# One unit's products walk their 512 columns in other orders

## The chip, the cores and the metric

The kernel runs on one core of a Trainium2 chip. The core has a matrix engine (TensorE, PE in the profile, with its weight loads as PEld), VectorE (DVE), ScalarE (ACT), GpSimd (POOL) and SyncE (SP), which here only issues loads and stores. The metric is the device time of one execution in microseconds (us); lower is better.

## The reference

The input is one sequence of 256 positions with 4096 features. The reference computes one layer and a last norm:

```python
xn = rms_norm(x, norm_attn)
q, k, v, g = split(xn @ w_in, 4)            # w_in: 4096 x 16384, 32 heads of 128
z = q @ k.T * scale                          # strictly causal
a = exp(log_sigmoid(z) + suffix sums of log_sigmoid(-z))
h = x + ((a @ v) * silu(g)) @ w_out          # w_out: 4096 x 4096
out = rms_norm(h, final_norm)
```

Nearly all of the work is in the two large products, xn @ w_in and the one with w_out. The convolution layer named in the reference's description isn't reached, since it runs for a depth of one.

## The kernel before, in words

**Units and steps.** The columns of w_in are cut into sixteen units (u = 0 to 15) of 1024 columns each: two blocks of 256 for q and k, two for gate and v. Four more units do w_out. A unit runs over the 4096 rows of the weights in sixteen steps (s = 0 to 15) of two chunks of 128 rows. In one step, a 2 x 2 block product has to be made: two halves of the rows of x, two chunks of the sum, and two groups of 512 columns.

**Seven or eight products.** Unit 0 makes eight products in each step. In every other unit the steps in `SEVEN` (1, 3, 4, 6, 7, 9, 10, 12, 13, 14) use a scheme of seven products with sums and differences of blocks, and the others (0, 2, 5, 8, 11, 15) use eight. So a unit after the first has 10 x 7 + 6 x 8 = 118 products. The results are gathered in seven accumulators of the PSUM memory (tiles `acc`, 128 partitions x 512 columns of fp32, one bank each), which stay open over the sixteen steps of a unit.

**A product is three matmuls.** An operand in fp32 is split into a high part, rounded to the format fp32r, and the remainder, also fp32r. `mm3` (line 762) then issues high x high, high x low and low x high, all into the same accumulator. The stationary operand, 128 x 128, is a part of x (tiles `sh`, `sl`; for w_out `oh`, `ol`); the moving operand, 128 x 512, is a part of the weights (tiles `wh`, `wl`). `mm3` is called by `product` (line 1185), which looks up the accumulator, the form of x and the piece of the weights.

**What feeds it.** SP loads the raw weights by 256 KB into seven buffers (`raw`), POOL adds a chunk onto some of them by a DMA that accumulates, VectorE makes further sums there, ScalarE writes `wh` (`piece`, line 426), and VectorE writes `wl`. In memory the 512 columns of `wh` and `wl` lie next to each other, in straight order, as do those of an accumulator. The buffers of `wh` and `wl` are returned when the product that used them last is done.

**The heads.** The attention of unit u's two heads (`head`, line 777) runs during the first seven steps of unit u + 1. Its matmuls (tiles `tr`, `z`, `o`) stand between the products in TensorE's order; at some places they are plain fp32, at others fp32r.

**What sets the order.** A planner written in the kernel (`Plan`, line 102) simulates the five engines with fixed costs while the program is built, and writes the instructions out in the order that comes of it. It reckons a product at three matmuls of `tensor_ns(512)`, whatever its operands look like. The order is therefore fixed before the kernel runs; on the chip the engines wait for one another by semaphores.

Of the kernel before, what the change touches and what calls it, by code (L numbers as in the profile page):

```python
# [84 lines left out]
def plain_part(k, one, two):  # L85

    return k, BOTH, ((one, "A11", 0), (two, "A21", 0), (one, "A12", 1), (two, "A22", 1))


def vector_ns(n):  # L90
# [147 lines left out]
def kernel(  # L238
# [41 lines left out]
    for u, (kind, w, cols) in enumerate(units):  # L280
        for s in (step_at(u, k) for k in range(NS)):
            quads.append(tuple((w, c, s) for c in cols))
            if kind == "plain":
                which = [plain_part(0, PLAIN["C11"], PLAIN["C21"]), plain_part(1, PLAIN["C12"], PLAIN["C22"])]
            else:
                which = SEVEN_PARTS if s in SEVEN and not (u == LAST and s in EIGHT_LAST) else EIGHT_PARTS
            for i, (k, place, prods) in enumerate(which):
                parts.append(
                    dict(u=u, s=s, i=i, tile=(len(quads) - 1, k), place=place, prods=prods, quad=len(quads) - 1,
                         seven=which is SEVEN_PARTS, size=place.stop - place.start)  # L290
                )
# [8 lines left out]
    for g, (n, k) in enumerate(order):  # L300
        p = parts[n]
        b = p["u"], p["prods"][k][0]
# [456 lines left out]
        nc.give("qkl")  # L759
        nc.tell(("gate", u))  # L760

    def mm3(out_, a, b, start, stop):

        (ah, al), (bh, bl) = a, b
        kw = dict(skip_group_check=True)
        nc.tensor.matmul(out_, ah, bh, start=start, stop=False, **kw)
        nc.tensor.matmul(out_, ah, bl, start=False, stop=False, **kw)
        nc.tensor.matmul(out_, al, bh, start=False, stop=stop, **kw)
# [416 lines left out]
    def product(n, k):  # L1185
        p = parts[n]
        b, f, c = p["prods"][k]
        h, l = forms[p["s"]]
        mm3(
            ev[p["u"]][b],  # L1190
            (h[:, PLACES[f], :], l[:, PLACES[f], :]),
            (wh[n][:, c, :], wl[n][:, c, :]),
            starts[p["u"], b] == (n, k),
            ends[p["u"], b] == (n, k),
        )

    def products():
        for g, (n, k) in enumerate(order):
            p = parts[n]
            u, s = p["u"], p["s"]  # L1200
            b, f, c = p["prods"][k]
            if u < 1:
                what = "s"
            elif u < OUT0:
                what = "n"
            elif u == OUT0:
                what = "o"
            else:
                what = "r" if u == LAST and s in EIGHT_LAST else "p"
            if starts[u, b] == (n, k):  # L1210
                yield nc.take(f"b{b}")
                ev.setdefault(u, {})[b] = acc.tile([P, W], F32, tag=f"b{b}", name=f"acc{u}_{b}")
            yield nc.until(("low", n, c), ("form", what, s), lead=nc.LEAD)
            yield nc.work(
                "tensor", PRODUCT, lambda: product(n, k), g * PRODUCT, after=lambda n=n, k=k: done(n, k), hold=False
            )
            nc.here = g * PRODUCT
# [59 lines left out]
```

## Time and profile before

| what | value |
|---|---|
| median of 3 runs | 1740.17 us (1738.72 to 1741.6) |
| span of the profiled execution | 1738.8 us |
| TensorE busy | 1722.9 us (99%) |
| VectorE busy | 1643.5 us (95%) |
| ScalarE busy | 1204.9 us (69%) |
| GpSimd busy | 335.5 us (19%) |
| mean granted TensorE clock | 0.998 |
| DMA | 413.79 MB, mean 238 GB/s |

For the profiled execution the page has the span, from the first to the last instruction, and no other time; it lies at the low end of the three runs. Busy time counts an engine's records. The records of matmuls overlap, since matmuls are pipelined: one of 512 columns is drawn with 389 ns, but they start closer together. What a matmul costs TensorE is therefore read from the distance between starts, or from a stretch that holds a known number of them. Nearly every instruction carries line 121, which is the helper that records it; groups are told apart by their tiles.

### The profile page before, as it was taken

How to read it: one execution, taken by the hardware profiler on the slowest of the kernel's cores; microseconds unless marked ns; L12 is line 12 of the kernel's file. 1: busy time of each engine (PE TensorE's matmuls, PEld its weight loads, DVE VectorE, ACT ScalarE, POOL GpSimd, SP SyncE). 2: the span in 40 equal slices, each digit the busy share in tenths (PEclk: the TensorE clock that was granted, in tenths of full speed). 3: DMA queues.
4: the chain of work that ended last, by engine and by line, in shares of the span. 5: the costliest groups of instructions: out<-in, count | busy, mean ns of one | idle time of the engine just before them, and what ended most of it. 6: DMA issues, size and time to landing. Idle time of an engine off the chain costs nothing.

```text
span 1738.8 us, 24830 instructions
## 1 busy us (share of the span) xinstructions
PE 1722.9 (99%) x7735; PEld 1412.5 (81%) x7735; DVE 1643.5 (95%) x2106; ACT 1204.9 (69%) x1640; POOL 335.5 (19%) x407
## 2 busy tenths in 40 slices
PE   9999999999999999999999999999999999999997
PEld 6888888888888888888888888888888888878885
DVE  8889999999999999999999999999999987999997
ACT  7976767676767676767676767676767675666655
POOL 0022222222222221212222222222222112221220
PEclk9999999999999999999999999999999999999999
DMA  9967788878787878787878787878787878788895
GB/s 363 297 191 227 229 231 226 230 229 236 224 234 223 240 216 238 217 251 208 255 206 255 206 256 198 257 203 259 198 256 203 269 245 265 230 268 251 233 303 191
DMA packets 249380, 413.79 MB, mean 238 GB/s; under 512 B 28128, under 2 KB 73440, under 8 KB 249248
## 3 DMA queue, kind: packets, MB, share of 16 engines
q1 hardware_dynamic: 194544, 354.24, 60.6%
q0 software_dynamic: 54416, 57.70, 20.2%
q8 instruction: 60, 0.98, 0.2%
q14 instruction: 72, 0.59, 0.1%
q10 hardware_dynamic: 288, 0.28, 0.0%
HBM read 403.98 MB, written 8.13 MB: 237 GB/s over the span
## 4 chain that ended last, share of the span: by engine, by line
PE 78%; DVE 12%; issue 6%; ACT 2%; DMA 2%; SPq 0%; DVEq 0%; ACTq 0%
PE acc L121 74%; DVE wl L121 8%; DVE raw L121 3%; PE z L121 2%; PE o L121 1%; ACT wh L121 1%; DMA raw<-in_w_in_dram 1%; PE tr L121 1%; DVE gv_sb L121 1%; DVE h L121 0%; DMA raw<-in_w_out_dram 0%; DMA grow<-in_gain_out_dram 0%; DVE qk_sb L121 0%; SPq L121 0%; ACT sq L121 0%
## 5 line engine op out<-in xcount | busy, mean ns | idle before, releaser
L121 ACT CAST wh<-raw 128x1024 fp32r<-128x1024 f32 (+1 forms) x995 | 922.0, 971 | 406.1 <-issue 180.0
L121 DVE TENSOR_TENSOR wl<-raw,wh 128x1024 fp32r<-128x1024 f32 (+1 forms) x995 | 1068.8, 1123 | 58.4 <-ACT wh L121 56.6
L121 PE MATMUL acc<-wh,sh 128*128 128x512 f32 x1898 | 755.6, 398 | 0.0
L121 PE MATMUL acc<-wl,sh 128*128 128x512 f32 x1898 | 740.0, 390 | 0.8 <-DVE wl L121 0.8
L121 PE MATMUL acc<-wh,sl 128*128 128x512 f32 x1898 | 740.5, 390 | 0.0
L121 POOL DMA_DIRECT2D raw<-in_w_in_dram x300 | 262.9, 988 | 1078.9 <-DMA raw<-in_w_in_dram 427.4
L121 PEld LDWEIGHTS acc<-wh,sl 128*128 128x128 f32 x1898 | 356.3, 188 | 75.8 <-DVE sl L121 0.4
L121 PEld LDWEIGHTS acc<-wl,sh 128*128 128x128 f32 x1898 | 357.0, 188 | 73.8 <-DVE wl L121 2.8
L121 PEld LDWEIGHTS acc<-wh,sh 128*128 128x128 f32 x1898 | 356.8, 188 | 70.7 <-ACT wh L121 0.6
L121 DVE TENSOR_TENSOR raw<-raw,raw 128x512 f32<-128x512 f32 x354 | 243.4, 687 | 6.9 <-DMA raw<-in_w_out_dram 1.2
L121 PE MATMUL acc<-wl,oh 128*128 128x512 f32 x485 | 189.7, 391 | 2.0 <-DVE wl L121 1.8
L121 PE MATMUL acc<-wh,oh 128*128 128x512 f32 x485 | 190.0, 392 | 0.0
L121 PE MATMUL acc<-wh,ol 128*128 128x512 f32 x485 | 188.9, 389 | 0.0
L121 DVE TENSOR_TENSOR raw<-raw 128x512 f32<-128x512 f32 x177 | 121.0, 684 | 0.0
L121 PEld LDWEIGHTS acc<-wl,oh 128*128 128x128 f32 x485 | 91.1, 188 | 23.8 <-DVE wl L121 5.3
L121 PEld LDWEIGHTS acc<-wh,oh 128*128 128x128 f32 x485 | 91.0, 188 | 19.2 <-DVE gv_sb L121 0.5
L121 PEld LDWEIGHTS acc<-wh,ol 128*128 128x128 f32 x485 | 91.0, 188 | 18.8
L121 POOL DMA_DIRECT2D raw<-in_w_out_dram x54 | 47.1, 968 | 185.9 <-DVE wl L121 58.9
L121 ACT ACTIVATE f<-f 128x384 f32<-128x384 f32 x96 | 50.5, 526 | 3.0
L121 ACT COPY qkT<-tr 128x512 f32<-128x512 f32 x32 | 18.6, 581 | 24.1 <-PE tr L121 24.1
L121 ACT CAST oh<-p 128x512 fp32r<-128x512 f32 (+3 forms) x46 | 20.9, 467 | 18.8 <-DVE p L121 13.2
L121 DVE SCALAR_TENSOR_TENSOR gv_sb<-acc,rin_v,gv_sb 128x512 f32<-128x512 f32 x45 | 33.4, 741 | 0.0
(91 smaller groups left out, 750.3 us busy)
## 6 DMA issues: line engine op xcount, KB each, us to landing
raw<-in_w_in_dram SPq DMA_DIRECT2D x1024, 256.0 KB, 4.5
raw<-in_w_out_dram SPq DMA_DIRECT2D x256, 256.0 KB, 4.3
raw<-in_w_in_dram POOLq DMA_DIRECT2D x300, 128.0 KB, 4.7
p<-spill POOLq DMA_DIRECT2D x28, 256.0 KB, 4.2
raw<-in_w_out_dram POOLq DMA_DIRECT2D x54, 128.0 KB, 5.1
xr<-in_x_dram SPq DMA_DIRECT2D x16, 256.0 KB, 4.8
xres<-in_x_dram SPq DMA_DIRECT2D x16, 256.0 KB, 5.6
out_dram<-h SPq DMA_DIRECT2D x16, 256.0 KB, 2.8
```

The costliest lines, as they stand in the source:

```text
L121: return self.tc.keep_in_program_order(getattr(self.engine, name)(*args, **kw))
```

## The change

The matmuls of one unit of w_in, unit 5, go over their 512 columns in another order. `WALKS` gives fourteen of the sixteen steps a pattern (h, e); steps 0 and 5 have none. `mm3` cuts the 512 columns into h equal parts, and each part into runs of e columns. The walk takes the first run of each part in turn, then the second run of each, and so on. The moving operand and the accumulator are both walked so, and each column of the product is added where it was added before. What lies in memory, and the stationary operand, stay as they are.

For pattern (2, 2), for example, the columns come as 0, 1, 256, 257, 2, 3, 258, 259 and so on; for (2, 128) as 0 to 127, 256 to 383, 128 to 255, 384 to 511.

```diff
+WALKED = 5
+WALKS = {
+    1: (2, 16), 2: (2, 8), 3: (2, 4), 4: (2, 2), 6: (2, 32), 7: (2, 64), 8: (2, 128),
+    9: (4, 16), 10: (8, 16), 11: (16, 16), 12: (32, 4), 13: (4, 4), 14: (8, 4), 15: (4, 64),
+}
...
-    def mm3(out_, a, b, start, stop):
+    def mm3(out_, a, b, start, stop, walk=None):
 
         (ah, al), (bh, bl) = a, b
+        if walk:
+            h, e = walk
+            out_, bh, bl = (t.rearrange("p (h i e) -> p i h e", h=h, e=e) for t in (out_, bh, bl))
         kw = dict(skip_group_check=True)
         nc.tensor.matmul(out_, ah, bh, start=start, stop=False, **kw)
         nc.tensor.matmul(out_, ah, bl, start=False, stop=False, **kw)
...
             starts[p["u"], b] == (n, k),
             ends[p["u"], b] == (n, k),
+            WALKS.get(p["s"]) if p["u"] == WALKED else None,
         )
```

## The prediction

> **What bounds the kernel now.** I read the page first: the engine totals, the slices, and the chain of work that ended last.
>
> ```profile
> span 1738.8 us, 24830 instructions
> PE 1722.9 (99%) x7735; PEld 1412.5 (81%) x7735; DVE 1643.5 (95%) x2106; ACT 1204.9 (69%) x1640; POOL 335.5 (19%) x407
> PEclk9999999999999999999999999999999999999999
> PE 78%; DVE 12%; issue 6%; ACT 2%; DMA 2%; SPq 0%; DVEq 0%; ACTq 0%
> ```
>
> TensorE is busy 99% of the span at the full granted clock, and 78% of the chain is its own work. VectorE, at 95%, is close behind, so I have to see which of the two sets the pace in the edited unit. I found unit 5 by counting products in program order: unit 0 has 128, every later input unit 118, each three matmuls. The windows view for units 4, 5 and 6, and then for steps 7 to 15 of unit 5 (columns: length, then busy time and instructions of each engine, granted clock, DMA share, GB/s):
>
> ```profile
> core 0: us, PE busy (x) PEld busy (x) DVE busy (x) ACT busy (x) POOL busy (x), PEclk, DMA share, GB/s
> 353.26:439.37 86.11, 86.11 (x391) 70.81 (x391) 82.96 (x103) 60.48 (x80) 18.24 (x22) 1.00 0.82 230
> 439.37:525.43 86.06, 86.06 (x391) 70.81 (x391) 82.93 (x103) 60.43 (x80) 18.01 (x21) 1.00 0.80 228
> 525.43:611.57 86.14, 86.14 (x391) 70.82 (x391) 82.98 (x103) 60.41 (x80) 17.95 (x22) 1.00 0.82 230
> 480.54:525.43 44.89, 44.89 (x199) 37.12 (x198) 42.69 (x50) 28.63 (x35) 10.97 (x13) 1.00 0.85 252
> ```
>
> Unit 5 takes 86.06 us, like its neighbours, and in it TensorE is never idle while VectorE has 3.1 us to spare. The waits inside unit 5 that concern TensorE are these (total us, times, longest):
>
> ```profile
> PEld z L121 <- DVE fl L121: 0.3, 1, 0.3
> PEld o L121 <- ACT gated L121: 0.3, 1, 0.3
> PEld tr L121 <- DVE gated L121: 0.2, 1, 0.2
> PEld o L121 <- issue: 0.2, 1, 0.2
> ```
>
> All of them belong to attention heads, and together they are 1.0 us; no product waits for its weights. The chain over the unit, with start, length and content of each piece, gives the price of a matmul:
>
> ```profile
> 21 pieces in order of time: start us, us, what
> ...
> 443.41 12.28 PE acc L121 x54
> ...
> 462.69 0.44 PE tr L121 x4
> ...
> 480.04 46.04 PE acc L121 x203
> ```
>
> The last row is 203 matmuls back to back: 46.04 / 203 = 226.8 ns for one walk over 512 columns. That pitch, not the 389 ns by which a record is drawn, is the price. So a nanosecond put on a matmul here is a nanosecond on the end.
>
> **The change part by part.** No instruction is added, removed or moved: in the lists of the two built kernels the only rows that differ, on any engine, are 306 matmuls of unit 5, which carry shapes such as 128x128x2x2 in place of 128x512. So no DMA, semaphore, queue or buffer changes its place. Each pattern (h, e) walks 512 columns as runs of e neighbours, going round h places that lie 512/h columns apart; operand and accumulator walk alike, so the sums are the same. Steps 0 and 5 have no pattern. Of the other fourteen, ten have 7 products (21 matmuls) and four (2, 8, 11, 15) have 8 (24 matmuls): 210 + 96 = 306, and 306 x 226.8 = 69.4 us of the path are touched.
>
> By run length: e = 2 in step 4 (21 matmuls, 256 runs each); e = 4 in steps 3, 12, 13, 14 (84 matmuls, 128 runs); e = 8 in step 2 (24, 64 runs); e = 16 in steps 1, 9, 10, 11 (87, 32 runs); e = 32, 64, 128 in steps 6, 7, 15, 8 (90, of 16 to 4 runs). That is 5,376 + 10,752 + 1,536 + 2,784 + 792 = 21,240 runs.
>
> The trace has no TensorE row whose moving operand or accumulator jumps. The nearest rows:
>
> ```profile
> L121 DVE TENSOR_TENSOR raw<-raw 128x512 f32<-128x512 f32 x177 | 121.0, 684 | 0.0
> L121 DVE TENSOR_TENSOR h<-acc,h 128x512 f32<-128x512 f32 x19 | 12.5, 681 | 0.0
> L121 PEld LDWEIGHTS acc<-wh,sl 128*128 128x128 f32 x1898 | 356.3, 188 | 75.8 <-DVE sl L121 0.4
> L121 PE MATMUL tr<-ident,qk_sb 128*128 128x128 f32 x128 | 19.2, 272 | 0.0
> ```
>
> On VectorE the first row reads and writes two runs of 256 columns that lie apart, the second one straight run out of the accumulator: 684 against 681 ns. A jump after a long run costs at most 3 ns there. That is the lower end, and I take it (as nothing) for long runs, e of 16 to 128. The LDWEIGHTS row says that the next weights take 188 of the 226.8 ns and lie beside the stream; they are read straight as before, and a slower stream only hides them better.
>
> The upper end is a stream at half rate. The last row is a transpose of plain fp32, 128 columns; four of them, in the chain above (tr x4), take TensorE 0.44 us, which is 440 ns for 512 columns, 213 ns more than the fp32r walk. I use it for whatever may feed or accept only half as much. A gain is bounded too: if these fp32 columns take the array two cycles, one cycle is 0.43 ns, 512 of them 220 ns, and the fp32r walk loses 6.8 ns to something else. Were a jump to remove that everywhere, it would give 306 x 6.8 = 2.1 us.
>
> Is there a limit near? Short fp32r streams stand in the timeline of a head:
>
> ```profile
> 455.53 0.33 PE L121 MATMUL z<-fh,neg_tri 128*128 128x384 f32 x1
> 455.70 0.34 PE L121 MATMUL z<-fl,neg_tri 128*128 128x384 f32 x1
> 455.88 0.22 PE L121 MATMUL z<-fh,neg_tri 128*128 128x128 f32 x1
> 455.94 0.28 PE L121 MATMUL z<-fl,neg_tri 128*128 128x128 f32 x1
> ```
>
> From start to start, 384 columns take 0.17 us and 128 columns 0.06: about 0.44 to 0.47 ns a column at every length, so the walk is paid by the column and not by the instruction. A stream that is slightly slower than the array's own 0.43 looks like one held by what feeds 4-byte columns. If that feed comes in pieces of a few columns, runs shorter than a piece waste part of it. The width of a piece is in no row. I choose that it is wider than 2 and not wider than 4: step 4, with the shortest runs, gets the half-rate row, and all others the row of the free jump, which they resemble more. The sum: 21 x (440 - 227) = 4.5 us in step 4, 0 elsewhere.
>
> [...]
>
> Nothing covers the 4.5 us: TensorE is the path in unit 5. What is late next gains slack: the splits on ScalarE and VectorE, the loads on SP's queue and the adding loads on POOL's are released by products of the same order, somewhat later, and then have 4.5 us more. At most the 1.0 us of waits above can come back inside the unit; I count none. Unit 6 has no idle TensorE either, so it gives nothing back. The sum on the profiled execution is 1738.8 + 4.5 = 1743.3 us. Its span is at the low end of the three runs (1738.72, 1740.17, 1741.6); on their median, 1740.17, it is 1744.7 us.
>
> **The rivals.** *No walk costs anything (the other side).* The place is step 4: if the feed delivers any aligned pair at full rate, the 4.5 us are gone, and the time is 1740.2 us, or down to 1738.1 with the bound of the gain. It decides from a pitch in step 4 under about 390 ns (3.5 us in 21 matmuls, which is 0.2%). For it speaks the 684 against 681; against it, that this row has a jump in 256 columns and runs at 1.3 ns a column, a third of TensorE's demand.
>
> *Short runs cost more widely.* If a piece is 8 columns, e = 4 falls to half rate too: 105 matmuls x 213 = 22.4 us, 1762.5 us. If every run costs one column's time (0.443 ns), 21,240 x 0.443 = 9.4 us, 1749.6 us. For it: the 6.8 ns lost in a straight walk show that the feed has no room. Against it: nothing shows how wide it is.
>
> *Every jump-ridden walk is slow.* If a walk that isn't one run loses the stream's full rate on the accumulator's side, whatever the run, all 306 pay: 306 x 213 = 65.2 us, 1805.4 us. For it: no row shows the accumulator written by TensorE in anything but straight order. Against it: in the steps with runs of 64 and 128 only 4 to 8 jumps per matmul would have to cost 213 ns.
>
> [...]
>
> *VectorE becomes the bound.* Only if the matmuls got more than 3.1 us faster in the unit; the bound of the gain is 2.1 us, so it doesn't.
>
> **How the numbers follow.** Only step 4 slow: 0.37 (1742 to 1750 us, a pitch in step 4 of some 315 to 690 ns). No cost: 0.27. Short runs wider: 0.20 (1745.8 to 1762.5). All slow: 0.13. A gain beyond 0.2%, by something that no row prices: 0.03. I predict the first, 1744.7 us. From 1738 to 1764 lie the first three, 0.84 less their tails. The runs before spread by 0.17%, so 0.2% (3.5 us) is about what can be told from no change. Slower: 0.37 + 0.20 + 0.13, less 0.03 for a mild step 4, is 0.67; same 0.27 + 0.03 = 0.30; faster 0.03.
>
> **What would show it.** In the changed kernel's timeline: matmuls of step 4 about 440 ns apart for 21 in a row (some 463 to 472 us from the start), and 227 ns in every other step; unit 5 about 90.5 us long and units 4 and 6 still 86.1; no new TensorE wait. I am wrong if step 8 (runs of 128) leaves 227 ns, if e = 4 does, or if step 4 doesn't.

## The result, and the profile after

The changed kernel takes 1745.15 us (median of 8 runs, 1743.9 to 1746.6) against 1739.24 us for the kernel before beside it (8 runs): the ratio is 1.0032, with a 95% interval of 1.0021 to 1.0042. That is 5.9 us more, and the forecast was 4.5 us more. The span of the profiled execution went from 1738.8 to 1744.0 us. The page's totals and chain of the changed kernel:

```profile
span 1744.0 us, 24830 instructions
PE 1727.7 (99%) x7735; PEld 1413.4 (81%) x7735; DVE 1644.3 (94%) x2106; ACT 1205.5 (69%) x1640; POOL 334.7 (19%) x407
...
PE 78%; DVE 11%; issue 5%; DMA 3%; ACT 2%; SPq 0%; DVEq 0%; ACTq 0%; POOL 0%; POOLq 0%
```

TensorE is still the bound, with the same number of instructions. The windows of units 4, 5 and 6, with the columns as before:

```profile
core 0: us, PE busy (x) PEld busy (x) DVE busy (x) ACT busy (x) POOL busy (x), PEclk, DMA share, GB/s
353.26:439.34 86.08, 86.08 (x392) 70.81 (x390) 82.95 (x102) 60.43 (x80) 18.19 (x22) 1.00 0.79 230
439.34:531.02 91.68, 91.68 (x391) 71.76 (x390) 85.18 (x104) 61.59 (x80) 18.06 (x21) 1.00 0.75 221
531.02:616.76 85.74, 85.74 (x392) 71.01 (x390) 81.78 (x100) 60.15 (x79) 18.04 (x21) 1.00 0.77 222
```

Unit 5 is 5.6 us longer, at the full clock; unit 6 is 0.4 us shorter; the others are as they were. In unit 5's chain the same pieces stand as before:

```profile
443.35 12.89 PE acc L128 x54
...
464.13 4.07 PE acc L128 x12
...
482.98 49.12 PE acc L128 x205
```

The middle row lies in step 4, with runs of two: 4.07 / 12 = 339 ns a matmul, not the 440 that I used. The last row covers the steps from 7 on, with a few matmuls of the neighbours at its ends: 49.12 / 205 = 239.6 ns, where I had put 226.8. In the timeline, step 4 first, then step 8 with its runs of 128, then step 14 with (8, 4):

```profile
465.99 0.51 PE L128 MATMUL acc<-wh,sh 128*128 128x512 f32 x1
466.33 0.51 PE L128 MATMUL acc<-wl,sh 128*128 128x512 f32 x1
466.67 0.51 PE L128 MATMUL acc<-wh,sl 128*128 128x512 f32 x1
...
489.23 0.39 PE L128 MATMUL acc<-wl,sh 128*128 128x512 f32 x1
489.45 0.39 PE L128 MATMUL acc<-wh,sl 128*128 128x512 f32 x1
489.68 0.39 PE L128 MATMUL acc<-wh,sh 128*128 128x512 f32 x1
...
519.76 0.45 PE L128 MATMUL acc<-wh,sh 128*128 128x512 f32 x1
520.04 0.45 PE L128 MATMUL acc<-wl,sh 128*128 128x512 f32 x1
```

The starts are 0.34 us apart in step 4, 0.22 to 0.23 in step 8 and 0.28 in step 14. From the starts of each step's first matmuls in both traces, the step lengths differ as follows (us; steps 1 to 6 hold heads too):

| e | steps and what each grew by | sum |
|---|---|---|
| 2 | 4: 2.17 | 2.17 |
| 4 | 3: 0.43, 12: 0.00, 13: 0.84, 14: 1.03 | 2.30 |
| 8 | 2: 0.39 | 0.39 |
| 16 | 1: 0.28, 9: 0.11, 10: 0.25, 11: 0.31 | 0.95 |
| 32 to 128 | 6: -0.04, 7: 0.02, 8: 0.00, 15: 0.02 | 0.00 |
| none | 0: -0.01, 5: -0.20 | -0.21 |

So of 5.6 us only 2.2 are in step 4. That the forecast of the time held was luck: step 4 was priced at twice its cost, the steps with runs of 4 to 16 at nothing, and the two errors largely cancel.

The zero of step 6 is no free walk. Its matmuls, with runs of 32, start some 238 ns apart, which is 0.2 us over the step. But of TensorE's waits at the heads, one of 0.3 us stood in step 5 and one in step 6 before, and both are gone after; so step 6 doesn't grow, and step 5, which has no pattern, is 0.20 us shorter.

### The profile page after: what moved, and what is told of

It is laid out like the page before. It is cut to its first block, busy times and chain, and to the rows that moved or that the text cites. A ratio compares the mean times of both kernels' runs of the same rounds, so it can differ in the third digit from the quotient of the medians.

```text
span 1744.0 us, 24830 instructions
## 1 busy us (share of the span) xinstructions
PE 1727.7 (99%) x7735; PEld 1413.4 (81%) x7735; DVE 1644.3 (94%) x2106; ACT 1205.5 (69%) x1640; POOL 334.7 (19%) x407
## 4 chain that ended last, share of the span: by engine, by line
PE 78%; DVE 11%; issue 5%; DMA 3%; ACT 2%; SPq 0%; DVEq 0%; ACTq 0%; POOL 0%; POOLq 0%
PE acc L128 73%; DVE wl L128 7%; DVE raw L128 2%; PE z L128 2%; ACT wh L128 2%; PE o L128 2%; DMA raw<-in_w_out_dram 1%; DMA raw<-in_w_in_dram 1%; PE tr L128 1%; DMA xres<-in_x_dram 1%; DVE h L128 1%; DVE gv_sb L128 1%; SPq L128 0%; DMA grow<-in_gain_out_dram 0%; DVE qk_sb L128 0%
## 5 line engine op out<-in xcount | busy, mean ns | idle before, releaser
L128 POOL DMA_DIRECT2D p<-spill x28 | 17.6, 702 | 78.4 <-DVE ol L128 67.9
```

What stands on the lines that cost most here:

```text
L128: return self.tc.keep_in_program_order(getattr(self.engine, name)(*args, **kw))
```

## The experiments

**Which side pays, and does the traffic around it matter?** The first kernel is TensorE alone, a loop of its own over operands of either type (fp32r and the 2-byte bf16), sides and patterns. The other three are the changed kernel with patterns spread over the units 1 to 15; `MOVING` and `INTO` say which side is walked (the lines that set them and the patterns are left out):

```python
for x, m in ((xh, wh), (xb, wb[:, 0:W])):
    for moving, into in ((True, True), (True, False), (False, True)):
        for h, e in PATTERNS:
            mm(x, m, h, e, moving, into, TIMES)
```

```diff
-            out_, bh, bl = (t.rearrange("p (h i e) -> p i h e", h=h, e=e) for t in (out_, bh, bl))
+            walked = lambda t: t.rearrange("p (h i e) -> p i h e", h=h, e=e)
+            straight = lambda t: t.rearrange("p (i h e) -> p i h e", h=h, e=e)
+            out_ = (walked if INTO else straight)(out_)
+            bh, bl = ((walked if MOVING else straight)(t) for t in (bh, bl))
...
-            WALKS.get(p["s"]) if p["u"] == WALKED else None,
+            WALKS.get((p["u"], p["s"])),
```

> A short kernel with nothing but matmuls of 512 columns on TensorE, each pattern 12 times in a row, into four accumulators in turn: for fp32r and for bf16 operands, first operand and accumulator walked alike, then the moving operand alone walked (accumulator straight), then the accumulator alone. It leaves out the whole computation of the reference. Theory 1 (the feed of the moving operand works in pieces of a few 4-byte columns): the first two blocks of fp32r show the pitches of the changed kernel, about 338 ns for (2, 2), 254 to 277 for e = 4, 240 for e = 8 and 16, 227 for e of 64 and more, and the third block shows 227 ns throughout; bf16, with half the bytes per column, shows less in each pattern. Theory 2 (the accumulator's side pays): the first and third blocks slow alike, the second at 227 ns, and bf16 pays as much as fp32r. Theory 3 (both are right, but only beside the traffic of the other engines): all blocks at about 227 ns except perhaps e = 2.

> The changed kernel with a pattern in steps 7 to 15 of the units 1 to 15 instead of unit 5 alone: 28 patterns, each in four or five places, the rest straight; steps 1 to 6 straight. If the pattern alone sets the pitch, the places of a pattern agree within some 2 ns, and the pitches of the changed kernel come back: (2, 2) 338, (2, 4) 254, (4, 4) 266, (8, 4) 277, (32, 4) 225, (2, 16) 240, (2, 64) and more 227. If other engines' traffic has a part, the places of one pattern differ by 5 ns or more, as the 226 to 242 ns inside the step of (4, 16) hint.

> The same places and patterns as both_sides, with the walk on the moving operand alone; the accumulator is gone through straight, so the columns of the products land in other places and the result is not the reference's. Theory 1 (feed of the moving operand): the pitches of both_sides. Theory 2 (accumulator): 227 ns in all.

> The same places and patterns, with the walk on the accumulator alone; the columns of the products land in other places, so the result is not the reference's. Theory 1: 227 ns in all. Theory 2: the pitches of both_sides. If both sides have a part, each of the two runs shows some of the excess, and I would look whether they add.

The times are 1928.49 us for both_sides, 1929.28 for moving_only and 1739.9 for accumulator_only, beside 1740.05 for the kernel before (one run each). One place, step 15 of unit 3 with pattern (4, 2), in the timelines of moving_only and then of accumulator_only:

```profile
393.15 0.63 PE L131 MATMUL acc<-wh,sl 128*128 128x512 f32 x1
393.59 0.63 PE L131 MATMUL acc<-wh,sh 128*128 128x512 f32 x1
394.03 0.63 PE L131 MATMUL acc<-wl,sh 128*128 128x512 f32 x1
```

```profile
348.95 0.39 PE L131 MATMUL acc<-wl,sh 128*128 128x512 f32 x1
349.18 0.39 PE L131 MATMUL acc<-wh,sl 128*128 128x512 f32 x1
349.41 0.39 PE L131 MATMUL acc<-wh,sh 128*128 128x512 f32 x1
```

Reading the moving operand in this order costs 444 ns a matmul; writing the accumulator in it costs nothing (0.23 us from start to start). That held for all 28 patterns: every pattern's median with the accumulator alone walked was 227 or 228 ns, and moving_only repeated both_sides in all but a few places. Theory 1 stands on that point, theory 2 falls. Theory 3 falls too, since TensorE alone shows the cost as well, in most patterns within 2 ns of the full kernel. Pitches in ns, from the distances between starts (in alone the median of twelve, in both_sides the means of the pattern's places):

| e | h | fp32r alone | bf16 alone | fp32r in both_sides |
|---|---|---|---|---|
| 2 | 2, 4, 8, 16 | 340, 443, 487, 440 | 271, 438, 435, 430 | 333-339, 443-445, 488-552, 439-478 |
| 2 | 32, 64, 128 | 431, 460, 451 | 460, 451, 226 | 431-440, 459-461, 450-453 |
| 4 | 2, 4, 8 | 250, 269, 278 | 227, 223, 218 | 250-251, 267-268, 278 |
| 4 | 16, 32, 64 | 243, 225, 232 | 216, 229, 226 | 246, 224-226, 231-233 |
| 8 | 2, 4, 8, 16, 32 | 244, 231, 234, 230, 232 | 216 | 243, 231-232, 249-257, 231-232, 234 |
| 16 | 2, 4, 8, 16 | 240, 233, 240, 241 | 216 | 240-242, 233-234, 240-241, 240-241 |
| 32 | 2, 4, 8 | 236, 233, 236 | 216 | 237, 234, 236-237 |
| 64, 128 | 2, 4; 2 | 230, 227; 227 | 216 | 229, 227-228; 227 |
| straight | | 227 | 216 | 227-229 |

Three things were not expected. The number of runs does not set the price: (8, 4) and (32, 4) both have 128 runs, at 278 and 225 ns. Next, bf16 with runs of 2, half as many bytes, still takes 430 ns or more in five of seven patterns, and in (32, 2) it takes more than fp32r, against the last clause of theory 1. And the pattern alone does not fix the pitch: the places of one pattern differ by 6 ns in (2, 2), 7 in (8, 8), 38 in (16, 2) and 64 in (8, 2). Other engines' traffic isn't needed for that, since (2, 2) settled at 340 ns in alone and at 328 in addresses, the next run, which is also TensorE alone. What picks the pitch is not settled.

**Do the addresses set the price?** Again TensorE alone, with the moving operand's access written out as [step, count] pairs (the loops around these lines are left out):

```python
PROBES.append(("straight", base, [(1, 512)]))
PROBES.append(("step", 0, [(k * e, 512 // e), (1, e)]))
PROBES.append(("pair4", 0, [(4, 64), (d, 2), (1, 4)]))
PROBES.append(("pair2", 0, [(2, 128), (d, 2), (1, 2)]))
```

> A short kernel with matmuls alone, straight accumulators, and moving operands read from one fp32r tile of 4096 columns in chosen orders, seven times each; it leaves out the computation of the reference. It asks what sets the pitch: the number of jumps or where they go. Orders: straight from several starts; runs of e columns at a fixed step of 0 to 8 runs; and two places d columns apart read in turn in runs of 4, 2 or 8. Theory A (each run shorter than a piece pays a fixed price for the jump): the pitch depends on e alone, e.g. about 250 ns for every d at e = 4 and 340 ns at e = 2. Theory B (addresses fall into banks that are busy for some time after an access): the pitch depends on d with a period, up to about 440 ns at the worst d of e = 4 and down to 216 ns (what bf16 took in the run alone) at the best; reading one place over and over (step 0) is as slow as the worst; and a fixed step of 2 or 4 runs of 4 columns falls into fewer banks and is slower than 227 ns. What has already been seen, 443 ns for (4, 2) with fewer places than (32, 2) at 431 and 225 ns for (32, 4) with as many jumps as (8, 4) at 278, speaks for B.

Two places d columns apart, read in turn: with runs of 4, d = 4 (neighbouring runs, so that nearly every column is read twice) took 215 ns, and nearly all other d 238 to 247. Near multiples of 64 columns it rose, most of all just behind them: 260 ns at d = 68, 132 and 196. With runs of 2, d = 4 gave 218 and all others 327 to 330, but 347 at 60 and 346 at 124. Runs of 4 at a fixed step took 227, 232, 227, 225, 267, 320, 234 and 253 ns for steps of 4, 8, 12, 16, 20, 24, 28 and 32 columns. One place over and over took 218 ns in runs of 2 and 4, not the worst as theory B had it (244 in runs of 16). Straight reads from a multiple of 64 columns took 227 ns (those from 128 only from the sixth matmul on), and most other starts 230 to 236. So neither theory holds as written: a fixed price per jump (A) is refuted by the steps, and the plain banks of B by the single place. Where the next run lies matters, with a period of 64 columns. The mechanism under it stays open.

**Is step 4 the whole of it?**

> The changed kernel with step 4 straight again, the other thirteen patterns left. By the prediction's sum all of the cost is in step 4, and unit 5 would be back at 86.1 us. By the pitches in the changed kernel's trace step 4 costs 21 x (338 - 227) = 2.3 us, and the other patterns some 3.3: unit 5 would be 91.7 - 2.3 = 89.4 us long.

```diff
-    1: (2, 16), 2: (2, 8), 3: (2, 4), 4: (2, 2), 6: (2, 32), 7: (2, 64), 8: (2, 128),
+    1: (2, 16), 2: (2, 8), 3: (2, 4), 6: (2, 32), 7: (2, 64), 8: (2, 128),
```

Unit 5 in the windows view of this kernel:

```profile
439.55:529.03 89.48, 89.48 (x391) 71.57 (x390) 84.72 (x104) 61.56 (x80) 18.03 (x21) 1.00 0.82 228
```

The unit shrank from 91.68 to 89.48 us, so step 4 costs 2.2 us, and 3.4 us over the straight 86.06 remain. My sum is refuted, the pitches are confirmed: each adds on its own.

**Can an order be faster than straight, and does the kernel get it?** In both_sides (32, 4) was under the straight pitch. I searched further orders with TensorE alone, and walked all products of the kernel as (32, 4):

> The same kind of short kernel as addresses, with further orders of the moving operand, seven times each: every (h, e) with e of 4 to 32 from four starts, the same with one or both digits going down, rows of two chunks lying interleaved, runs of e columns with 4 to 32 columns left out between them, and straight runs going down. If a straight read loses its 11 ns against bf16 at every border of 64 columns because of the order in which the banks come round, some padded or turned order should stand at 216 to 220 ns; if the feed is simply that slow, the best stays at 224 to 225 as in (32, 4). Starts off a multiple of 64 columns: 230 ns and more, as in the run addresses.

> Every fp32r product of the kernel walked as (32, 4), the one pattern that was under the straight pitch (224 ns in four of five places of both_sides, 226 in the fifth, against 226.7). If TensorE's pitch sets the time throughout, 7149 x (226.7 - 224.4) = 16 us are gained, 1723 us, and a unit is 85.3 us long. VectorE is busy 82.9 us of a unit's 86.1, so it should not stop this; if its waits come up all the same, or if most places are at 226 ns, the gain is under 5 us.

```diff
+WALK = (32, 4)
...
-            WALKS.get(p["s"]) if p["u"] == WALKED else None,
+            WALK,
```

In orders, nothing reached 216 to 220 ns on the average. (32, 4) had 222 to 224 from three of four starts, with single values from 218 to 230, and 226 from the fourth. With its runs taken from last to first it was 222.1, always 221 to 224. Straight runs going down were slower, 230 to 234. all_32_4 took 1737.63 us against 1740.21, ratio 0.9985 (0.9976 to 0.9994): 2.6 us gained instead of 16. In its trace steps 8 to 13 settle either near 223.3 ns or to a repeating row of 220, 222, 221, 234, 239, 225, 226 with the mean 226.7, and once in one of them a unit mostly stays there. Next, the turned order in all products, and with TensorE alone narrower stationary operands:

> A short kernel with matmuls alone, accumulators straight, twelve orders of the moving operand 32 times each, with stationary operands of 128, 64 and 32 columns; it leaves out the computation of the reference. It asks what the pitch of a straight fp32r read, 226.7 ns against 216 in bf16, is made of. Theory A (the moving stream alone sets it): no pitch changes with the stationary's width. Theory B (the next weights are read through the same memory in the meantime and take turns from it): with 64 and 32 columns the straight pitch falls towards 216 ns, and the changing pitches inside one order, such as 218, 230, 224, 221 of (32, 4), settle to one value; the loss of (2, 2), 340 ns, falls too, by no more than some 10 ns.

> Every fp32r product walked as (32, 4) with the four runs of each part taken from the last to the first, operand and accumulator alike; in the run orders this was 222.4 ns with no matmul outside 221 to 224, while (32, 4) going up came to 226.7 on the average of most steps in all_32_4. If that pitch holds in the kernel, a product's matmul is 4.3 ns shorter, 7149 x 4.3 = 31 us, and VectorE, 82.9 us busy in a unit that would then be 84.6 long, begins to be waited for: between 1709 and 1722 us. If the matmuls fall into a repeating pattern of the straight pitch's mean here as well, 1736 to 1740 us.

The edit of all_down, against all_32_4:

```diff
+def turned(t, h, e):
+    i = W // (h * e)
+    dims = [list(t.ap[0]), [-e, i], [W // h, h], [1, e]]
+    return dataclasses.replace(t, offset=t.offset + (i - 1) * e, ap=dims)
...
-            out_, bh, bl = (t.rearrange("p (h i e) -> p i h e", h=h, e=e) for t in (out_, bh, bl))
+            out_, bh, bl = (turned(t, h, e) for t in (out_, bh, bl))
```

With 64 stationary columns (32, 4) settled at 220.0 ns instead of 226.7 and (2, 2) at 326.7 instead of 333.3, so theory A does not hold as written. It isn't shown that the loading of weights does this: a narrower stationary operand also writes fewer rows of the accumulator, and (2, 2) ran at 328 ns with 128 columns too, in addresses (d = 256), and at 338 with 32 columns. The straight read did not fall (226.7, 230.0 and 231.7 ns with 128, 64 and 32 columns), against theory B. What limits a straight read to 226.7 ns is not settled.

all_down took 1737.27 us against 1740.26, ratio 0.9983 (0.9974 to 0.9992): again 3 us of 31. Some of its units ran steps 7 to 13 at 222.2 ns, some at 226.7, and yet, in units 2 to 13, both kinds are 85.8 to 86.2 us long. Unit 7, one of the fast ones, in the windows view, then its longest wait of TensorE, and the page's chain by engine:

```profile
609.66:695.47 85.81, 85.10 (x391) 70.61 (x390) 82.72 (x102) 60.43 (x80) 18.36 (x22) 1.00 0.80 234
```

```profile
PEld acc L132 <- DVE wl L132: 0.8, 1, 0.8
```

```profile
PE 41%; DVE 29%; issue 16%; DMA 6%; ACT 6%; SPq 1%; DVEq 0%; ACTq 0%; POOL 0%; POOLq 0%
```

TensorE now idles for 0.7 us in the unit, a product waits 0.8 us for the `wl` that VectorE writes (0.4 in unit 7 before), step 14 has a mean of 252 ns, and VectorE's share of the chain went from 12% to 29%. To see whether VectorE took the gain, I halved its sums of raw weights in two kernels, the one before and all_down:

```diff
-                lambda: nc.vector.tensor_tensor(out=to[:, :, at_, :], in0=f, in1=g, op=op), W,
+                lambda: nc.vector.tensor_tensor(out=to[:, 0:1, at_, :], in0=f[:, 0:1], in1=g[:, 0:1], op=op), W,
```

> The kernel before, straight walks, with the three sums that VectorE makes of raw weights in each seven-product step done on half of their columns; the other half is left as loaded, so the result is not the reference's, and the planner's order is the same. VectorE has about 8 us less to do in a unit (30 sums, each some 270 ns shorter). If TensorE alone sets the kernel before, a unit stays at 86.0 to 86.1 us and the time at 1740 us; what the heads wait for VectorE, 1 us a unit, may shrink a little.

> The kernel of all_down (every product walked as (32, 4) with the runs from last to first) with the same halved sums, so again not the reference's result. If in all_down VectorE's chain took back what the faster steps gained, units in which steps 7 to 13 go at 222 ns are now 84.5 to 85.2 us long instead of 85.8 to 86.0, without the slow step 14, and the time is 1715 to 1728 us. If the gain is lost in TensorE's own stream (the steps at 226.7 ns on the average), it stays within 2 us of all_down's 1737 us.

They took 1727.6 and 1700.95 us (one run each, beside 1742.5 for the kernel before). The pages of half_sums and then of down_half_sums, and unit 7 of the latter:

```profile
span 1725.9 us, 24988 instructions
PE 1711.7 (99%) x7735; PEld 1417.5 (82%) x7735; DVE 1519.7 (88%) x2106; ACT 1208.1 (70%) x1640; POOL 334.6 (19%) x407
...
PE 99%; DVE 1%; DMA 0%; ACT 0%; issue 0%; DVEq 0%; SPq 0%; ACTq 0%
```

```profile
span 1699.3 us, 24990 instructions
...
PE 96%; DVE 2%; DMA 1%; issue 1%; ACT 1%; SPq 0%; DVEq 0%; ACTq 0%
```

```profile
600.63:684.54 83.91, 83.91 (x392) 71.04 (x390) 75.72 (x101) 60.04 (x79) 17.28 (x22) 1.00 0.83 233
```

With VectorE relieved, the turned walk is worth 26.6 us (1727.6 to 1700.95); with VectorE as it is, 3.0. In down_half_sums every input unit from unit 3 on lasts 83.91 us and its steps 8 to 15 stay at 222.2 ns, and unit 7 lists no wait of TensorE; time and units came out below what was expected of it (1715 to 1728 and 84.5 to 85.2 us). So VectorE's chain took back nearly all of the gain, and the waits for it seem to be what moved the matmuls between the two paces. That last part is only argued. half_sums itself went past its expectation: the units are 85.58 us and the span falls from 1738.8 to 1725.9 us, so VectorE already cost the kernel before some 0.5 us in a unit, and more outside those units. TensorE's busy time had hidden that (86.06 of 86.06 us in unit 5), since records of 389 ns also cover starts that come later than 227 ns.

## Why the prediction was right or wrong

*TensorE's stream in unit 5 is the path, with nothing to cover a slower matmul.* Right in the main: 5.6 us more in the unit became 5.2 in the span. TensorE's waits, of which I counted none, did give way, from 1.0 to 0.2 us in unit 5. "It gives nothing back" was slightly wrong for unit 6, which is 0.4 us shorter, with heads' waits down from 1.0 to 0.3 us. That VectorE had got ahead during the slow steps would explain both; it was not tested.

*The limit is the feed of the moving operand.* Right as to the side: moving_only has all of the cost (1929.28 us, against 1928.49 with both sides walked), accumulator_only none (1739.9, against 1740.05 before).

*Step 4 at a half-rate stream, 4.5 us.* Over-sized: 339 ns, 2.2 us. With two places in turn the half rate was not seen; with four or more, runs of two took 431 to 552 ns, (4, 2) 443.

*Nothing elsewhere.* Wrong; this is the step that failed. I put the width of a piece between 2 and 4 columns and gave every longer run the price of VectorE's free jump. Runs of 4, 8 and 16 cost 3.6 us together, and only from 64 on the jump was nearly free (227 to 230 ns). No other width saves the idea of a piece: (16, 16) has runs of 16 and costs 14 ns a matmul, (32, 4) has runs of 4 and, at 224 to 226 ns, costs nothing. What stands in its place, that the address of the next run matters, is a finding without a mechanism. VectorE's row at 1.3 ns a column says nothing on a stream that wants a column every 0.44 ns. The rival of wider costs for short runs came closest, but its two prices fail as well: a fixed price per run would make (8, 4) and (32, 4) alike, and half rate at e = 4 was seen in no pattern (h, 4), 278 ns being the most.

*No gain beyond 2.1 us in the unit.* The bound held here, where the best step, (32, 4), came out even. Its 6.8 ns a matmul was a fair bound as well: the turned (32, 4) saves 4.5, and the most seen in a whole step, (16, 8) at 220.0 ns in step 7 of unit 3 in moving_only, 6.7.

*VectorE has 3.1 us to spare in a unit.* Wrong as a reading. That sum of idle pieces was not slack: all_down shows VectorE taking the place of the bound after less than 1 us, and half_sums that it already held the unit back by 0.5.

*The accumulator rival.* Refuted for what was run: 28 patterns on the accumulator, all with runs of two or more, left 227 to 228 ns a matmul in accumulator_only. Single columns were not tried.

## What to carry to other kernels

In the patterns tried here, a strided fp32r moving operand is not free on TensorE even in runs of 16 columns (5 to 15 ns on 227), nearly doubles the matmul or more in six of seven patterns with runs of two (431 to 487 ns alone), and is nearly free from 64 columns on (227 to 230 ns); the accumulator was walked in runs of two or more at no cost (227 to 228 ns). A total that comes out right is no proof of its terms: compare the step that was to cost something, and those that were to cost nothing, one by one. Before working on the bound engine, give the next one less to do in a throwaway kernel: here the same walk was worth 3 us or 27 (the latter from one run of each kernel), depending on VectorE.

## What was not expected

An order of reading can beat the straight one: 222.2 ns for (32, 4) with its runs turned, against 226.7. The same instructions settle into one of two paces, 222.2 or 226.7 ns (223.3 or 226.7 for (32, 4) going up), and keep it for whole steps. Other orders do so too: (16, 8) took 219 and 221 ns in turn through the whole of one step of moving_only, and 231 on the average in its other places. A straight fp32r read is itself slower than bf16 (226.7 against 216 ns) with TensorE alone, and no order of 512 different columns closed that gap.
